# Moving the scale and offset of a norm behind the spatial mix of a gMLP layer

## The chip, the cores and the metric

The kernel runs on one core of a Trainium2 chip. The metric is the device time of one execution in microseconds (us). The engines are named as in the profile: PE multiplies matrices (TensorE), PEld loads its weights, DVE is the vector engine, ACT the scalar engine, POOL is GpSimd, and SP issues nearly all DMAs, in the order of its queue. Each engine works through its own queue in order and waits on semaphores for the others.

## The reference

The program is one inference step of a two-layer decoder, for a prompt of 512 tokens and 8 samples of 8 tokens (576 columns in all), model width 1024. Layer 0 has two attention groups, layer 1 a gMLP; each is followed by a feed-forward network with a short convolution. Only the gMLP matters here:

```
z = gelu(h @ w_in)                              # 1024 -> 4096 columns
u, v = split(z, 2, axis=-1)                     # 2048 each
v = (v - mean(v)) * rsqrt(var(v) + eps) * g + b     # g, b: one per feature (lnv_g, lnv_b)
vg = v.reshape(B, T // 128, 128, 8, 256)        # chunks of 128 positions, 8 groups of features
mixed = einsum('gts,bnsgc->bntgc', w_s * tri, vg) + b_s.T[:, :, None]
out = (u * mixed) @ w_out
```

`w_s` is a causal 128x128 matrix for each group. The normalised v (with g and b) of the 64 sample tokens is an output as well.

## The kernel before

All matrix products with weights are made of three matmuls of halves: weights and activations are split into a rounded part (`wh`, `xh`) and the rest (`wl`, `xl`). For a tile of weights, SP loads `wr` (line 250), ACT rounds it to `wh` (line 251), and DVE or POOL subtracts to get `wl` (line 254); in the gMLP layer it is always DVE. Each of the three kinds has three buffers. Columns of tokens are worked in two parts, 0 to 255 and 256 to 575.

The function `gmlp` (line 548) runs in these stages:

- The mixing weights `ws` (prompt) and `wq` (samples) are loaded and masked by POOL (line 560), the bias `bs` is loaded.
- v is projected with tokens on partitions, in eight column blocks c of 256 (lines 572 to 602). ACT writes the GELU into `z` (128 partitions, 5 blocks of tokens, 2048 features), DVE takes statistics.
- The norm of v (lines 603 to 613): `moments` (line 446) turns the statistics into mean `mv` and inverse deviation `r` by Newton steps on DVE; then, for each of four column blocks of 512 and five token blocks, DVE subtracts and scales (line 610), DVE multiplies by the gain `gb[:, 0]` (611) and POOL adds the offset `gb[:, 1]` (612). The sample rows go out as `o_cv` (613).
- `left(c)` (line 617) projects a block of 128 features of u for all tokens: 48 matmuls of line 298 into two accumulators `acc`, each read by ACT with a GELU (621). `right(c)` (line 623) mixes the same 128 features of z over positions on PE (lines 630 and 632), adds the bias on DVE (635), multiplies by u (637), and splits the product into `gch` on ACT (740) and `gcl` on DVE (741).
- `out` (line 642) multiplies four such blocks by `w_oc` and adds to the residual `x` (line 439).

Three `left`s run ahead of the first `right`. The accumulators `acc` are a ring of four banks; the two loads `gb` have two buffers. What the order on each engine is, a scheduler decides ahead of time from its own model of durations; a call of `late` pins an instruction behind the one before it on its engine. On PE it placed the first mixes into the fourth `left`.

Of the kernel before, what the change touches and what calls it, by code (L numbers as in the profile page):

```python
# [10 lines left out]
F32 = mybir.dt.float32  # L11
F32R = mybir.dt.float32r
I32 = mybir.dt.int32
AF = mybir.ActivationFunctionType
OP = mybir.AluOpType
# [3 lines left out]
P = 128  # L19
# [3 lines left out]
NS = 64  # L23
# [15 lines left out]
GB = 2  # L39
# [163 lines left out]
class Net:  # L203
# [344 lines left out]
    def gmlp(self, x, last, psum, pool, xp, *norm):  # L548

        nc, a, xs, xn = self.nc, self.a, last.xs, last.xn  # L550
        g1 = self.plus_one(1, 2, xp, "g1")

        ws = pool.tile([P, 8, P], F32, name="ws")
        wq = pool.tile([NS, 8, NS], F32, name="wq")
        for t, src, mask in ((ws, "wsT", "c_triT"), (wq, "wsS", "c_triB")):
            n = t.shape[0]
            self.late(nc.sync.dma_start(t, a[src]))
            tri = xp.tile([P, T], F32, name="tmp", bufs=3)[:n, :n]
            self.late(nc.sync.dma_start(tri, a[mask]))
            nc.gpsimd.tensor_tensor(t, t, tri[:, None, :].to_broadcast([n, 8, n]), op=OP.mult)  # L560
        bs = pool.tile([P, 8, P], F32, name="bs")
        self.late(nc.sync.dma_start(bs, self.rows(a["bs"], P).rearrange("p (g t) -> p g t", g=8)))

        z = pool.tile([P, 5, 2 * D], F32, name="z", bufs=1)
        st = pool.tile([P, 5, 8, 6], F32, name="zst")
        self.late(nc.gpsimd.memset(st[NS:, 4], 1.0))
        self.late(nc.gpsimd.memset(z[NS:, 4], 0.0))
        todo = [(c, u) for c in range(8) for u in range(2)]
        led = {}

        def lead():
            c, u = todo.pop(0)
            if u == 0:
                led[c] = [], [psum.tile([P, 2, 256], F32, name=name, bufs=b) for name, b in (("acc", 4), ("tc", 2))]
            units, accs = led[c]
            units.append(self.weights(a["w_v"][c, u], 1024))
            self.token_unit({tb: accs[tb // 4][:, tb % 2] for tb in (2, 3, 4)}, units[u], u, 256, xs, xn, True, (2, 3, 4))


        for _ in range(3):  # L580
            lead()
        for c in range(8):
            first = None
            for u in range(2):
                if c not in led or u == len(led[c][0]):
                    lead()
                units, accs = led[c]
                first = first or psum.tile([P, 2, 256], F32, name="acc", bufs=4)
                self.token_unit([first[:, 0], first[:, 1]], units[u], u, 256, xs, xn, True, (0, 1))
            accs = [first] + led.pop(c)[1]  # L590
            for i in range(3):
                n, nb = (P, 2) if i < 2 else (NS, 1)
                zz = z[:n, 2 * i:2 * i + nb, c * 256:c * 256 + 256]
                if i < 2:
                    nc.scalar.activation(zz, accs[i], AF.Gelu)
                else:
                    self.both_halves(accs[i][:, 0], zz[:, 0])
                    nc.scalar.activation(zz, zz, AF.Gelu)
                for t in range(nb):
                    nc.vector.bn_stats(st[:n, 2 * i + t, c], zz[:, t])  # L600
            if c == 0:
                last.residual()
        mv, r = self.moments(st, pool)
        for c in range(4):
            gb = pool.tile([P, 2, 512], F32, name="gb", bufs=GB)
            self.late(nc.sync.dma_start(gb[:, 0], self.rows(a["lnvg"][:, c * 512:(c + 1) * 512], P)))
            self.late(nc.sync.dma_start(gb[:, 1], self.rows(a["lnvb"][:, c * 512:(c + 1) * 512], P)))
            for tb in range(5):
                zz = z[:, tb, c * 512:(c + 1) * 512]
                nc.vector.tensor_scalar(zz, zz, mv[:, tb, 0:1], r[:, tb:tb + 1], op0=OP.subtract, op1=OP.mult)  # L610
                nc.vector.tensor_tensor(zz, zz, gb[:, 0], op=OP.mult)
                nc.gpsimd.tensor_tensor(zz, zz, gb[:, 1], op=OP.add)
        nc.sync.dma_start(a["o_cv"], z[:NS, 4])
        mm = nc.tensor.matmul
        u = {}

        def left(c):
            wh, wl, _ = self.weights(a["w_u"][c], 1024)
            u[c] = pool.tile([P, T], F32, name="u", bufs=UA + 1)
            for part, (t0, t1) in enumerate(PARTS):  # L620
                nc.scalar.activation(u[c][:, t0:t1], self.product(psum, wh, wl, 0, xs, part), AF.Gelu)

        def right(c):
            cols = slice(c * P, (c + 1) * P)
            g = c // 2
            gt = xp.tile([P, T], F32, name="tmp", bufs=3)
            for part, (t0, t1) in enumerate(PARTS):
                mix = psum.tile([P, 512], F32, name="acc", bufs=4)
                for n in range(2):
                    mm(mix[:, n * P:(n + 1) * P], z[:, 2 * part + n, cols], ws[:, g], start=True, stop=True)  # L630
                if part:
                    mm(mix[:, 256:256 + NS], z[:NS, 4, cols], wq[:, g], start=True, stop=True)
                for o, i, n, m in ((t0, 0, 2, P), (NP, 256, 8, 8))[:1 + part]:
                    wide = lambda t: t.rearrange("p (n t) -> p n t", n=n)
                    nc.vector.tensor_tensor(wide(gt[:, o:o + n * m]), wide(mix[:, i:i + n * m]),
                                            bs[:, g, None, :m].to_broadcast([P, n, m]), op=OP.add)
            nc.vector.tensor_mul(gt, gt, u.pop(c))
            pair = tuple(t[:, c % GC] for t in ring)
            self.split_to(*pair, gt)
            return self.halves(pair)  # L640

        def out(*chunks, norm=None):
            self.accumulate(x, a["w_oc"], [(c0, [gc.pop(c) for c in range(c0, c1)]) for c0, c1 in chunks],
                            g1, psum, xp, None, norm)

        ring = self.pair(pool, [P, GC, T], "gc")
        gc = {}
        for c in range(UA):
            left(c)
        for c in range(16):  # L650
            if c + UA < 16:
                left(c + UA)
            gc[c] = right(c)
            for c0, c1 in GO[0]:
                if c1 == c + 1:
                    out((c0, c1))
        norm = Norm(self, x, *norm, psum, pool, xp, "z")
        out(*GO[1], norm=norm)
        return norm
# [862 lines left out]
def _layout(inp):  # L1522
    n = lambda k: np.asarray(inp[k])
    fm = lambda w, cols: w.reshape(w.shape[0] // P, P, w.shape[1] // cols, cols)
    d = {}
    x = np.concatenate([n("x_prompt")[0], n("x_sample").reshape(NS, D)], 0)
    d["xT"] = x.T.reshape(KB, P, T).transpose(1, 0, 2)
    c = np.concatenate([n("c_prompt"), n("c_sample")], 0)
# [13 lines left out]
    o = dict(qa=0, ka=512, va=1024, qi=1536, sm=2048, qb=2120, kb=2632, vb=3144, fb=3656)  # L1542
# [21 lines left out]
    ws = n("w_spatial")[0]  # L1564
    d["wsT"] = ws.transpose(2, 0, 1)
    d["wsS"] = np.tile(ws[:, :8, :8].transpose(2, 0, 1), (8, 1, 8))
    d["bs"] = n("b_spatial").reshape(1, 1024)
    d["lnvg"], d["lnvb"] = n("lnv_g"), n("lnv_b")
    for k, v in _consts().items():
        d["c_" + k] = v  # L1570
    return {k: np.ascontiguousarray(v) for k, v in d.items()}
# [41 lines left out]
```

## Time and profile before

| | |
|---|---|
| median of 3 runs | 1954.88 us (1953.62 to 1960.26) |
| profiled execution | 1954.99 us, span 1952.9 us |
| TensorE clock granted, mean | 0.968 |
| PE busy | 1830.8 us (94% of the span) |
| DVE busy | 1185.3 us (61%) |
| ACT busy | 736.5 us (38%) |
| POOL busy | 374.0 us (19%) |
| DMA | 284.39 MB, mean 146 GB/s |

The span runs from the first to the last instruction; the execution's own time is 2.1 us longer. Shares are averages over stages with different limits. The gMLP layer lies between about 1130 and 1510 us. Of the clock, 1.00 in a row stands for 2.4 GHz and 0.50 for 1.2 GHz.

### The profile page before, as it was taken

How to read it: one execution, taken by the hardware profiler on the slowest of the kernel's cores; microseconds unless marked ns; L12 is line 12 of the kernel's file. 1: busy time of each engine (PE TensorE's matmuls, PEld its weight loads, DVE VectorE, ACT ScalarE, POOL GpSimd, SP SyncE). 2: the span in 40 equal slices, each digit the busy share in tenths (PEclk: the TensorE clock that was granted, in tenths of full speed). 3: DMA queues.
4: the chain of work that ended last, by engine and by line, in shares of the span. 5: the costliest groups of instructions: out<-in, count | busy, mean ns of one | idle time of the engine just before them, and what ended most of it. 6: DMA issues, size and time to landing. Idle time of an engine off the chain costs nothing. (4 is left out here: it accounts for less than half of the span.)

```text
span 1952.9 us, 37037 instructions
## 1 busy us (share of the span) xinstructions
PE 1830.8 (94%) x14456; PEld 1627.1 (83%) x14456; DVE 1185.3 (61%) x2437; ACT 736.5 (38%) x1372; POOL 374.0 (19%) x521
## 2 busy tenths in 40 slices
PE   6889999898889899999999999899998999999996
PEld 4646877555559899999999899799997999999995
DVE  3549963455449754545456953875468555565577
ACT  2323222255444533424344433122224535344543
POOL 2323511110025300100012330430013201010124
PEclk9989999999899999999999999899998999999998
DMA  8446587797864345353543333321222231313242
GB/s 287 128 151 219 179 263 244 238 304 240 279 232 141 118 132 181 126 181 128 193 140 109 107 101 98 94 70 59 82 97 86 71 103 62 102 50 114 87 139 92
DMA packets 140032, 284.39 MB, mean 146 GB/s; under 512 B 32338, under 2 KB 42002, under 8 KB 139794
## 3 DMA queue, kind: packets, MB, share of 16 engines
q1 hardware_dynamic: 139138, 279.67, 43.8%
q0 software_dynamic: 720, 2.36, 0.4%
q8 instruction: 114, 1.87, 0.4%
q14 instruction: 60, 0.49, 0.1%
HBM read 271.04 MB, written 10.94 MB: 144 GB/s over the span
## 5 line engine op out<-in xcount | busy, mean ns | idle before, releaser
L298 PE MATMUL acc<-xh,wh 128*128 128x256 f32 (+1 forms) x1664 | 499.9, 301 | 3.0 <-ACT xh L161 1.7
L298 PE MATMUL acc<-xl,wh 128*128 128x256 f32 (+1 forms) x1664 | 497.5, 299 | 4.8 <-DVE xl L162 4.8
L298 PE MATMUL acc<-xh,wl 128*128 128x256 f32 (+1 forms) x1664 | 496.0, 298 | 6.0 <-DVE wl L254 6.0
L251 ACT CAST wh<-wr 128x1024 fp32r<-128x1024 f32 (+2 forms) x276 | 260.7, 949 | 536.6 <-PE acc L298 371.6
L254 DVE TENSOR_TENSOR wl<-wr,wh 128x1024 fp32r<-128x1024 f32 (+2 forms) x211 | 229.4, 1090 | 240.2 <-ACT wh L251 214.4
L298 PEld LDWEIGHTS acc<-xh,wh 128*128 128x128 f32 x1664 | 319.9, 192 | 11.5 <-issue 6.2
L298 PEld LDWEIGHTS acc<-xh,wl 128*128 128x128 f32 x1664 | 319.9, 192 | 6.6 <-DVE wl L254 6.2
L298 PEld LDWEIGHTS acc<-xl,wh 128*128 128x128 f32 x1664 | 319.9, 192 | 6.2 <-DVE xl L162 6.0
L254 POOL TENSOR_TENSOR wl<-wr,wh 128x1024 fp32r<-128x1024 f32 x65 | 160.5, 2469 | 531.2 <-ACT wh L251 513.4
L298 PE MATMUL acc<-gh,wl 128*128 128x256 f32 (+1 forms) x704 | 207.7, 298 | 1.6 <-DVE wl L254 1.6
L298 PE MATMUL acc<-gl,wh 128*128 128x256 f32 (+1 forms) x704 | 208.8, 298 | 0.0
L298 PE MATMUL acc<-gh,wh 128*128 128x256 f32 (+1 forms) x704 | 207.5, 300 | 0.4 <-ACT gh L740 0.4
L439 DVE SCALAR_TENSOR_TENSOR x<-acc,g,x 128x256 f32<-128x256 f32 x256 | 119.7, 476 | 118.3 <-PE acc L298 112.9
L525 DVE SCALAR_TENSOR_TENSOR y<-up,wc,y 128x592 f32<-128x592 f32 x176 | 150.6, 856 | 34.0 <-ACT y L522 29.9
L298 PEld LDWEIGHTS acc<-gh,wh 128*128 128x128 f32 x704 | 132.4, 189 | 5.5 <-issue 2.9
L298 PEld LDWEIGHTS acc<-gh,wl 128*128 128x128 f32 x704 | 132.6, 189 | 2.9 <-DVE wl L254 1.9
L298 PEld LDWEIGHTS acc<-gl,wh 128*128 128x128 f32 x704 | 133.3, 189 | 0.3 <-DVE gl L741 0.2
L518 POOL COPY tail<-up 128x2 f32<-128x2 f32 x88 | 26.1, 297 | 519.4 <-ACT up L516 519.1
L516 ACT COPY up<-acc 128x256 f32<-128x256 f32 x176 | 65.1, 371 | 130.0 <-PE acc L298 121.8
L283 PE MATMUL s<-wh,xh 128*128 128x256 f32 (+1 forms) x256 | 82.4, 330 | 3.2 <-ACT wh L251 3.2
L522 ACT ACTIVATE y<-up,wc 128x592 f32<-128x592 f32 x88 | 77.8, 884 | 9.2 <-POOL up L514 1.1
L285 PE MATMUL s<-wh,xl 128*128 128x256 f32 (+1 forms) x256 | 81.0, 317 | 0.0
(435 smaller groups left out, 3513.5 us busy)
## 6 DMA issues: line engine op xcount, KB each, us to landing
wr<-in_w_up SPq DMA_DIRECT2D x88, 512.0 KB
wr<-in_w_down SPq DMA_DIRECT2D x32, 512.0 KB
wh<-in_w_mod SPq DMA_DIRECT2D x30, 512.0 KB
wl<-in_w_mod SPq DMA_DIRECT2D x30, 512.0 KB
wr<-in_w_mod SPq DMA_DIRECT2D x28, 512.0 KB
own<-in_kT_b SPq DMA_DIRECT2D x48, 256.0 KB
own<-in_v_b SPq DMA_DIRECT2D x44, 256.0 KB
wr<-in_w_down SPq DMA_DIRECT2D x32, 320.0 KB
```

The source lines that it names most:

```text
L251: nc.scalar.copy(h, r)
L254: (nc.vector if low == "v" else nc.gpsimd).tensor_sub(l, r, h.bitcast(F32))
L283: mm(out, sh, mh, start=start, stop=False)
L285: mm(out, sl, mh, start=False, stop=stop)
L298: mm(acc, w[:, k * P:(k + 1) * P], m, start=i == 0, stop=i == n - 1)
L439: nc.vector.scalar_tensor_tensor(xp, acc[:, :256], g1[:, ob, 0:1], xp, op0=OP.mult, op1=OP.add)
L516: nc.scalar.copy(u[:, 2 + 256 * part:258 + 256 * part], accs[part][:, :256])
L518: nc.gpsimd.tensor_copy(tail[:, blk, 0:2], u[:, NP:NP + 2])
L522: nc.scalar.activation(y[:, :n], u[:, 0:n], AF.Identity, bias=wc[:, 3, blk:blk + 1], scale=wc[:, 0, blk:blk + 1])
L525: nc.vector.scalar_tensor_tensor(y[:, :n], u[:, k:k + n], wc[:, k, blk:blk + 1], y[:, :n], op0=OP.mult, op1=OP.add)
```

## The change

Since g and b belong to a feature, they can be taken out of the sum over positions: mixing `n * g + b` over s gives `g * mix(n) + b * sum_s w[t, s]`. So `z` is now only centred and scaled. The normalization is shared by DVE (token blocks 0, 2, 4) and ACT (blocks 1 and 3, with a `shift` of -mean * r). Two matmuls of a tile of ones with the masked `ws` give the sums of the mixing weights on all partitions (`wsum`, copied out by ACT). In `right`, DVE forms for each block of 128 features an offset tile `off = wsum * b + bs`, and the bias sum becomes `mix * g + off`. The gains and offsets come a second time as `lnvT`, one per partition. The output `o_cv` is made apart on POOL, in eight pieces of 256 features for the 64 sample rows, with loads of g and b broadcast to 64 partitions and a store for each piece.

```
+        lnv = pool.tile([P, 2, 16], F32, name="lnv")
+        self.late(nc.sync.dma_start(lnv, a["lnvT"]))
...
+        one = pool.tile([P, P], F32, name="one")
+        self.late(nc.gpsimd.memset(one, 1.0))
+        wsum = pool.tile([P, 8, P], F32, name="wsum")
+        for i in range(2):
+            ps = psum.tile([P, 4, P], F32, name="acc", bufs=4)
+            nc.tensor.matmul(ps, one, ws[:, 4 * i:4 * i + 4], start=True, stop=True)
+            nc.scalar.copy(wsum[:, 4 * i:4 * i + 4], ps)
+
         mv, r = self.moments(st, pool)
+        shift = pool.tile([P, 5], F32, name="zshift")
+        nc.vector.scalar_tensor_tensor(shift, mv[:, :, 0], -1.0, r, op0=OP.mult, op1=OP.mult)
         for c in range(4):
-            gb = pool.tile([P, 2, 512], F32, name="gb", bufs=GB)
-            self.late(nc.sync.dma_start(gb[:, 0], self.rows(a["lnvg"][:, c * 512:(c + 1) * 512], P)))
-            self.late(nc.sync.dma_start(gb[:, 1], self.rows(a["lnvb"][:, c * 512:(c + 1) * 512], P)))
             for tb in range(5):
                 zz = z[:, tb, c * 512:(c + 1) * 512]
-                nc.vector.tensor_scalar(zz, zz, mv[:, tb, 0:1], r[:, tb:tb + 1], op0=OP.subtract, op1=OP.mult)
-                nc.vector.tensor_tensor(zz, zz, gb[:, 0], op=OP.mult)
-                nc.gpsimd.tensor_tensor(zz, zz, gb[:, 1], op=OP.add)
-        nc.sync.dma_start(a["o_cv"], z[:NS, 4])
+                if tb % 2:
+                    nc.scalar.activation(zz, zz, AF.Identity, bias=shift[:, tb:tb + 1], scale=r[:, tb:tb + 1])
+                else:
+                    nc.vector.tensor_scalar(zz, zz, mv[:, tb, 0:1], r[:, tb:tb + 1], op0=OP.subtract, op1=OP.mult)
+        for c in range(8):
+            cols = slice(c * 256, c * 256 + 256)
+            gb = pool.tile([NS, 2, 256], F32, name="gb", bufs=GB)
+            for i, name in enumerate(("lnvg", "lnvb")):
+                self.late(nc.sync.dma_start(gb[:, i], self.rows(a[name][:, cols], NS)))
+            nc.gpsimd.tensor_tensor(gb[:, 0], gb[:, 0], z[:NS, 4, cols], op=OP.mult)
+            nc.gpsimd.tensor_tensor(gb[:, 0], gb[:, 0], gb[:, 1], op=OP.add)
+            nc.sync.dma_start(a["o_cv"][:, cols], gb[:, 0])
...
             gt = xp.tile([P, T], F32, name="tmp", bufs=3)
+            off = pool.tile([P, P], F32, name="goff", bufs=2)
+            nc.vector.scalar_tensor_tensor(off, wsum[:, g], lnv[:, 1, c:c + 1], bs[:, g], op0=OP.mult, op1=OP.add)
...
-                    nc.vector.tensor_tensor(wide(gt[:, o:o + n * m]), wide(mix[:, i:i + n * m]),
-                                            bs[:, g, None, :m].to_broadcast([P, n, m]), op=OP.add)
+                    nc.vector.scalar_tensor_tensor(wide(gt[:, o:o + n * m]), wide(mix[:, i:i + n * m]), lnv[:, 0, c:c + 1],
+                                                   off[:, None, :m].to_broadcast([P, n, m]), op0=OP.mult, op1=OP.add)
```

The scheduler now sets another order in this stage; outside of the gMLP layer no engine's order changes. On DVE, behind the Newton steps, the order before was this (`wl<-wr,wh` are the remainders of the weights, `z<-z,mv,rsy` the normalization, `tmp<-acc,bs` the bias sum):

```order
L610 TENSOR_SCALAR z<-z,mv,rsy 128x512 x9
L611 TENSOR_TENSOR z<-z,gb 128x512
L610 TENSOR_SCALAR z<-z,mv,rsy 128x512 x5
L611 TENSOR_TENSOR z<-z,gb 128x512 x8
L610 TENSOR_SCALAR z<-z,mv,rsy 128x512
L611 TENSOR_TENSOR z<-z,gb 128x512
L610 TENSOR_SCALAR z<-z,mv,rsy 128x512 x5
L254 TENSOR_TENSOR wl<-wr,wh 128x1024 x2
L635 TENSOR_TENSOR tmp<-acc,bs 128x256
L254 TENSOR_TENSOR wl<-wr,wh 128x1024
```

Now the same place on DVE reads as follows (lines of the changed kernel, where 623 is the normalization, 616 the shift, 655 the scaled sum, 646 the offset tile):

```order
L616 SCALAR_TENSOR_TENSOR zshift<-mv,rsy 128x5
L623 TENSOR_SCALAR z<-z,mv,rsy 128x512 x12
L254 TENSOR_TENSOR wl<-wr,wh 128x1024 x3
L655 SCALAR_TENSOR_TENSOR tmp<-acc,lnv,goff 128x256
L254 TENSOR_TENSOR wl<-wr,wh 128x1024
L655 SCALAR_TENSOR_TENSOR tmp<-acc,lnv,goff 128x256
L655 SCALAR_TENSOR_TENSOR tmp<-acc,lnv,goff 128x64
L657 TENSOR_TENSOR tmp<-tmp,u 128x576
L646 SCALAR_TENSOR_TENSOR goff<-wsum,lnv,bs 128x128
L761 TENSOR_TENSOR gcl<-tmp,gch 128x576
```

The first `wl` now stands behind 12 instructions on z, before behind 30. On ACT, the two copies and the eight normalizations stand between the casts of `wh` for the third and the fourth `left`:

```order
L251 CAST wh<-wr 128x1024
L612 COPY wsum<-acc 128x512 x2
L639 ACTIVATE u<-acc 128x256
L621 ACTIVATE z<-z,zshift,rsy 128x512 x8
L251 CAST wh<-wr 128x1024
L639 ACTIVATE u<-acc 128x320
```

Before, the GELU and the casts stood there alone. On PE, the two matmuls for `wsum` come just ahead of the first `left`, and the first mix now comes behind the whole fourth `left`. On SP, the pieces of the new output stand between the loads of weights:

```order
L250 DMA wr<-in_w_u 128x1024 x6
L631 DMA o_cv<-gb 64x256
L628 DMA gb<-in_lnvg 64x256
L628 DMA gb<-in_lnvb 64x256
L631 DMA o_cv<-gb 64x256
L628 DMA gb<-in_lnvg 64x256
L628 DMA gb<-in_lnvb 64x256
L250 DMA wr<-in_w_u 128x1024
L250 DMA wr<-in_w_oc 128x512
L631 DMA o_cv<-gb 64x256
```

This pattern goes on up to the eighth `o_cv`, with three more single loads of `w_oc` in it; the fifth load of `w_oc` comes behind the eighth `o_cv`. Before, the same loads had two pairs of `gb` and one `o_cv` between them.

## Rows read from the trace of the kernel before

**Rows 1.** Busy time by stretch: stretch, its length, engines (instructions), clock, DMA share, GB/s

```profile
1130.00:1230.00 100.00, 100.00 (x808) 90.76 (x807) 46.38 (x79) 33.62 (x53) 15.54 (x12) 1.00 0.32 101
...
1250.00:1260.00 10.00, 3.97 (x24) 3.21 (x22) 10.00 (x8) 1.38 (x2) 10.00 (x7) 0.79 0.17 51
1260.00:1270.00 10.00, 7.42 (x44) 7.42 (x45) 9.97 (x11) 0.38 (x1) 6.13 (x5) 0.70 0.52 156
...
1280.00:1290.00 10.00, 7.83 (x44) 7.03 (x44) 9.23 (x11) 1.52 (x4) 5.64 (x4) 0.83 0.23 72
...
1300.00:1350.00 50.00, 50.00 (x376) 49.42 (x375) 26.56 (x59) 12.83 (x21) 0.00 (x0) 1.00 0.26 81
```

**Rows 2.** PE in order of time: start, duration, engine, line, operands, idle before

```profile
1231.96 0.28 PE L298 MATMUL acc<-xh,wh 128*128 128x256 f32 x1
...
1251.17 0.28 PE L298 MATMUL acc<-xh,wh 128*128 128x256 f32 x1
...
1252.83 0.49 PE L630 MATMUL acc<-ws,z 128*128 128x128 f32 x2 [0.52 <-POOL z L612]
1254.49 0.49 PE L630 MATMUL acc<-ws,z 128*128 128x128 f32 x2 [1.18 <-POOL z L612]
1255.90 0.69 PE L632 MATMUL acc<-wq,z 64*128 64x64 f32 x2 [0.92 <-POOL z L612]
1262.58 0.58 PE L298 MATMUL acc<-xh,wl 128*128 128x256 f32 x1 [6.00 <-DVE wl L254]
...
1286.64 2.34 PE L630 MATMUL acc<-ws,z 128*128 128x128 f32 x8 [2.17 <-DVE tmp L635]
...
1297.70 1.05 PE L630 MATMUL acc<-ws,z 128*128 128x128 f32 x8
...
1299.05 0.39 PE L298 MATMUL acc<-gch,wh 128*128 128x256 f32 x1
```

**Rows 3.** DVE in order of time, from the end of the Newton steps

```profile
1237.32 4.20 DVE L610 TENSOR_SCALAR z<-z,mv,rsy 128x512 f32<-128x512 f32 x9
...
1245.30 4.89 DVE L611 TENSOR_TENSOR z<-z,gb 128x512 f32<-128x512 f32 x8
...
1253.24 7.09 DVE L610 TENSOR_SCALAR z<-z,mv,rsy 128x512 f32<-128x512 f32 x5
1260.25 4.49 DVE L254 TENSOR_TENSOR wl<-wr,wh 128x1024 fp32r<-128x1024 f32 x2
...
1274.81 7.48 DVE L611 TENSOR_TENSOR z<-z,gb 128x512 f32<-128x512 f32 x5
```

**Rows 4.** POOL in order of time, the first stretch of its sums

```profile
1246.06 17.60 POOL L612 TENSOR_TENSOR z<-z,gb 128x512 f32<-128x512 f32 x9 [2.33 <-DVE z L611]
```

**Rows 5.** PE by stretch: length, busy (instructions), clock, DMA share, GB/s

```profile
1260.00:1262.00 2.00, 0.00 (x0) 0.50 0.01 5
...
1288.00:1290.00 2.00, 2.00 (x8) 0.50 0.75 229
```

**Rows 6.** POOL's lines 612 and 560: ns min/median/max, first and last start

```profile
L612 POOL TENSOR_TENSOR z<-z,gb x20: 1380/1727/5297, 1242.3 to 1283.4; 128x512 f32<-128x512 f32 x20
...
L560 POOL TENSOR_TENSOR wq<-wq,tmp x1: 1292/1292/1292, 1144.6 to 1144.6; 64x512 f32<-64x512 f32 x1
```

**Rows 7.** ACT by shape over the span: count, busy us, mean ns, idle before

```profile
L251 ACT CAST wh<-wr 128x1024 fp32r<-128x1024 f32 x204 | 213.3, 1048 | 366.8 <-PE acc L298 212.0 <-DMA wr<-in_w_aa 34.5 <-DMA wr<-in_w_v 30.8
...
L134 ACT ACTIVATE z<-z,shift,rsy 128x512 f32<-128x512 f32 x4 | 3.0, 808 | 3.2 <-DVE shift L124 3.2
```

**Rows 8.** An f32 matmul of 512 columns, and DVE's scaled sum from PSUM

```profile
L1122 PE MATMUL o<-relu,i_c_selh x16: 592/595/1219, 105.9 to 126.3; 128*128 128x512 f32 x16
...
L439 DVE SCALAR_TENSOR_TENSOR x<-acc,g,x 128x256 f32<-128x256 f32 x256 | 119.7, 476 | 118.3 <-PE acc L298 112.9
```

**Rows 9.** SP's queue: a load of gb, and the store of o_cv

```profile
1255.87 0.33 SPq L606 DMA_DIRECT2D gb<-in_lnvg  x1
...
1287.63 0.51 SPq L613 DMA_DIRECT2D o_cv<-z  x1
```

More of the change, by code (lines that the diff above doesn't have):

```diff
@@ L1568, in _layout @@
     d["lnvg"], d["lnvb"] = n("lnv_g"), n("lnv_b")
+    d["lnvT"] = np.stack([n("lnv_g"), n("lnv_b")], 1).reshape(2, 16, P).transpose(2, 0, 1)
     for k, v in _consts().items():
```

## The prediction

> **What bounds it now.** I read a table of busy time by stretch around the gMLP layer first [rows 1]. While v is projected (1130 to 1230) PE is busy for all 100 us at full clock; from 1300 it is again. So a change counts only where PE stands still or runs slow. Between them lie two holes: 3.97 us busy of 10 from 1250, and 7.83 of 10 from 1280, with clocks of 0.79, 0.70 and 0.83. In both, DVE is busy for 9 to 10 us of 10. Then PE in order of time [rows 2]. The u projections ("lefts") run from 1231.96. After 1251 the first spatial mix waits three times for POOL's z (0.52, 1.18, 0.92). At 1256 PE begins 6.00 us of waiting for wl of line 254, a DVE instruction, and at 1286.64 it has waited 2.17 us for DVE's tmp. Idle time sums to 10.79 us. Last DVE and POOL [rows 3, 4]. DVE's queue holds 20 subtractions and scalings of z (line 610) and 20 products with gb (611), and POOL 20 sums with gb (612). The wl that PE waits for stands behind them on DVE. POOL's running sums also stretch DVE: line 610 takes 4.20/9 = 0.47 us without POOL and 7.09/5 = 1.42 beside it.
>
> The price of the two holes is the gap between what PE had to do and the time it took, up to the first matmul of the output projection (gch, 1299.05). From 1231.96 that is 67.09 us. The work in it is seven lefts and four mixes (c = 0 to 3; three lefts run ahead). Three lefts undisturbed last 1251.17 - 1231.96 = 19.21, so one is 6.40; a mix is 1299.05 - 1297.70 = 1.35 [rows 2]. 7 x 6.40 + 4 x 1.35 = 50.2. So 16.9 us are lost: 10.8 idle, the other 6.1 mostly half clock. The clock stood at 0.50 (1.2 GHz) in the idle time at 1260 to 1262, and again at 1288 to 1290 behind the second wait [rows 5]; the work done in such stretches takes twice as long.
>
> **The change part by part.** *Removed from DVE:* 20 products of 0.61 (4.89/8) to 1.50 us (7.48/5) and 8 of 20 normalizations. Kept are 12 of 0.47, or 1.42 beside POOL [rows 3]. *Removed from POOL:* 20 sums over 128x512. Added are 16 operations over 64x256. The nearest row is 64x512 at 1.29 us [rows 6], so about 0.65 each, 10 us in all, and no mix depends on them.
>
> *Moved to ACT:* 8 normalizations. The same form (line 134) takes 0.808 [rows 7], 6.5 us in all, and two copies of 128x512, priced like that row, 1.6 at most.
>
> *Added on PE:* two f32 matmuls over 512 columns, ahead of the lefts. An f32 matmul is two passes in the trace (a mix has four and stands as x8 in rows 2). A pass at the pace of a left (24 matmuls of 576 columns in all in 6.40, 0.46 ns a column) is 0.24; the isolated row of that shape says 0.595 [rows 8]. Four passes are 0.9 to 2.4. I take 0.9, since PE is streaming there. Their two accumulators come from the same four banks and push the later ones on by two. PE went through those banks without a wait up to 1251 [rows 2], so I cost this at nothing; uncovered it is one read by ACT, 0.8 by rows 7. What they multiply, the masked weights, POOL makes long before, at about 1144 (line 560 [rows 6]). One load of 16 KB goes ahead of the w_v loads: nothing, since PE is busy through that whole stretch [rows 1].
>
> *Added on DVE:* 16 offsets of 128x128, two ahead of the normalization and 14 in the loop. Nearest is the 128x256 form, 0.476 [rows 8], so 0.25 to 0.48, 4 to 8 us over the loop, where DVE is busy 26.56 of 50 [rows 1]. Each stands before gcl, at a point where DVE waits for ACT's cast anyway: nothing. The bias sum becomes a scaled sum of the same size, also covered.
>
> *What is late next.* In the new order PE meets the mixes only after four whole lefts. Its times, with 0.9 us added: left 1 at 1239.3, left 2 at 1245.7, left 3 at 1252.1, first mix at 1258.5, output projection at 1283.1. DVE's Newton steps end at 1237.3 [rows 3]; two offsets and the new shift make it 1238.0. DVE: 12 x 0.47 ends at 1243.7 (all 12 beside POOL: 1255.0). ACT: 8 x 0.808 ends at 1244.5. Behind these stands the cast wh of left 3 on ACT (1.05 [rows 7]), 1245.6, and its wl on DVE (2.25 by row 1260.25 of rows 3, the dear case), 1247.9 against a need at 1252.1. Closer is an accumulator: the second part of left 2 reuses the bank of left 0's second part, whose GELU stands behind the cast on ACT: done 1246.0, needed at 1245.7 + 6.40 x 256/576 = 1248.6. Slack 2.6 us, the smallest I find. The mix needs z at 1258.5, 14 us after ACT is done.
>
> *Sum:* 16.9 - 0.9 = 16.0 us. The profiled execution took 1954.99 (span 1952.9 and 2.1 around it), 0.1 above the median of the runs. Forecast 1939.0.
>
> **Two rules weighed.** Beside POOL a normalization takes 1.42 us against 0.47 [rows 3]. The Trainium skill (SBUF — State Buffer, Who interferes with whom) says that a DVE copy, cast or tensor_scalar in a two-port mode and a GpSimd instruction shut each other out for a whole instruction, while one with at most one SBUF input does not contend. By that, each POOL operation under way costs one of the 12 normalizations at most its own length, and the new sum from PSUM costs nothing; the trace's 0.95 us of stretch beside 1.4 us sums agrees in size. It would make rival C real only if all POOL work falls into the 6 us.
>
> The gb loads of before, two of 256 KB issued from 1255.87 on, had left the engines nearly empty by 1260 to 1262 (DMA share 0.01): 4.1 us, and I use 4.4 with something for the signal [rows 5, 9]. The Trainium skill (DMA: Bandwidth & Descriptors, Rules for kernel authors) says that under 64 KB a transfer is mostly overhead, and its section on latency puts the fixed part at about 2 us. That speaks against cutting one store and eight loads into 24 transfers of 64 KB. By it a step of the chain below would be an estimated 1.3 + 1.3 + 2.0 = 4.6 us, where a landing of a quarter of the bytes in a quarter of the time would make it 3.7.
>
> **Rivals.** *A, the SP queue holds up the weights.* The o_cv chain now is 8 steps: gb loaded, POOL twice, o_cv out; SP issues in order, a gb waits behind the o_cv before it, and the w_oc loads stand between them. A step is three issues (0.33 to 0.51 each [rows 9], 1.0 to 1.5), two POOL operations (2 x 0.65 = 1.3, at worst half of the 17.60/9 = 1.96 of rows 4 each, 2.0) and a landing of 1.1 (a quarter of the bytes in a quarter of the 4.4 us) to 4.4. That is 3.4 to 7.9; I take 4.8 (1.3, 1.3, and half of the 4.4 for one of the two loads). The first o_cv can go at 1240.7, behind DVE's third normalization and two POOL operations; the eighth goes seven steps later, and the fifth w_oc right behind it. A unit of w_oc lasts half a left, 3.2 us, so the fifth is needed at 1283.1 + 12.8 = 1295.9, less some 4.5 for load (half of 4.4), cast and wl: issue by 1291.4. It decides from (1291.4 - 1240.7)/7 = 7.2 us a step; at 7.9 PE waits 4.6 us: 1943.6. For it: 24 transfers, each pair waiting for the one before. Against: 34 us at my value, 51 available. *B, ACT is late.* If the 8 normalizations took over 1.14 us each, PE would wait for the bank; at 1.5 by 2.9 us: 1942. The rows of that form average 0.808 [rows 7]. *C, DVE is stretched.* All 12 at 1.42 put wl of left 3 at 1257.3, 5 us late, and some 2 us of half clock after it: 1946. Only POOL operations of the first steps fall into that time, a few of 0.65. *D, the time is given back:* the output projection would run into its weights. From 1300 on DMA share is 0.26 and PE never starves [rows 1], so a shift of the start shifts the end; 1950 if two thirds came back. *E, the slower side:* the same chain as in A with POOL held off by DVE as at its worst. With POOL at 2.65 us an operation (half of the longest sum, 5.30 [rows 6]) a step is 1.3 + 5.3 + 4.4 = 11.0, and PE waits 77 - 51 = 26 us for w_oc in the middle of the projection: 1965. It is slower than before from (50.7 + 16)/7 = 9.5 us a step. POOL's 5.30 was met once in 20, with DVE's queue full of two-input products that are now gone.
>
> **Chances.** Forecast 0.80 (1935.5 to 1942); A 0.07; B 0.03; C 0.04; D 0.04; E 0.02. Range 1935 to 1946: below for a loss that I may have sized too small (its half-clock part is a remainder) and the spread of runs, above to A, B and C; D and E are left out. A measurement of this kernel can tell about 0.3%, 5.9 us, from no change, so "faster" is below 1949.0: the forecast, A, B and C, 0.94. "Same" is D, 0.04, "slower" E, 0.02.
>
> **What would show it.** Right: PE busy 10 of 10 at clock 1.00 from 1232 to 1300, the first gch matmul near 1283, four f32 passes before the first left of about 0.24 us each. DVE done with z near 1244 to 1246, ACT near 1245, no wait of PE for line 254 or for z. The o_cv steps 4 to 6 us apart on SP, the last before 1291. Wrong: a wait of PE for ACT's u in left 2 (B), for wl in left 3 (C), or for wl of w_oc with SP waiting for POOL (A, E); or the gch matmul early but the end not (D).

## The result and the profile after

The changed kernel takes 1943.09 us (median of 6 runs, 1936.08 to 1947.28) against 1954.56 (6 runs, 1950.94 to 1960.26): a ratio of 0.9937, 95% interval 0.9917 to 0.9956, or 12.3 us by the ratio. Taken again beside the experiments it gave 0.9925 (0.9904 to 0.9946). The forecast was 1939.0, the range 1935 to 1946.

The profiled execution took 1944.53 us. Its span divides at two matmuls on PE: the first one behind the v projection, and the first `gch` matmul of the output projection.

| us | before | after | difference |
|---|---|---|---|
| start of the span to the end of the v projection | 1231.96 | 1234.91 | +2.95 |
| from there to the first `gch` matmul ("the gap") | 67.09 | 52.17 | -14.92 |
| from there to the end ("the tail") | 653.85 | 655.72 | +1.87 |
| span | 1952.9 | 1942.8 | -10.1 |

The first line lies ahead of nearly all that was changed. In the ten profiles of this document it is anything from 1226.5 to 1234.9 us, so it is the spread of runs. The other two sum to 13.05 us, or 0.67%, within both intervals; the second is the change, and the third is taken up again in the part on the prediction.

The busy time by stretch of the kernel after, with the columns of [rows 1]:

```profile
1130.00:1230.00 100.00, 100.00 (x809) 91.17 (x808) 44.74 (x74) 32.58 (x51) 15.68 (x13) 1.00 0.29 94
...
1250.00:1260.00 10.00, 10.00 (x78) 10.00 (x77) 2.45 (x2) 3.00 (x6) 2.52 (x5) 1.00 0.43 118
1260.00:1270.00 10.00, 10.00 (x75) 9.81 (x74) 4.54 (x7) 2.44 (x4) 3.07 (x3) 1.00 0.22 65
1280.00:1290.00 10.00, 10.00 (x76) 9.81 (x76) 6.01 (x12) 2.69 (x5) 1.61 (x2) 1.00 0.31 89
1300.00:1350.00 50.00, 50.00 (x375) 49.25 (x374) 25.32 (x53) 12.92 (x22) 0.00 (x0) 1.00 0.22 71
```

Both holes are closed. DVE, busy for 9 to 10 us of 10 before, now is for 2.45 to 6.01. PE in order of time, to be held against [rows 2]:

```profile
1234.91 1.88 PE L611 MATMUL acc<-ws,one 128*128 128x512 f32 x4
1236.22 0.68 PE L298 MATMUL acc<-xh,wh 128*128 128x256 f32 x1
1236.74 0.28 PE L298 MATMUL acc<-xl,wh 128*128 128x256 f32 x1
...
1243.01 0.28 PE L298 MATMUL acc<-xh,wh 128*128 128x256 f32 x1
...
1262.21 1.05 PE L650 MATMUL acc<-ws,z 128*128 128x128 f32 x8
...
1287.08 0.38 PE L298 MATMUL acc<-gch,wh 128*128 128x256 f32 x1
```

From the first left to the first `gch` matmul no row of PE has a wait. The four passes for `wsum` take 1.31 us to the start of the next matmul, and that one's successor comes 0.52 later where the others come 0.12 apart: the first left lasts 6.79 us, the next ones 6.40. Now DVE (to be held against [rows 3]), ACT and POOL:

```profile
1240.72 6.41 DVE L623 TENSOR_SCALAR z<-z,mv,rsy 128x512 f32<-128x512 f32 x12
1247.58 1.22 DVE L254 TENSOR_TENSOR wl<-wr,wh 128x1024 fp32r<-128x1024 f32 x1 [0.45 <-ACT wh L251]
...
1265.86 0.82 DVE L646 SCALAR_TENSOR_TENSOR goff<-wsum,lnv,bs 128x128 f32<-128x128 f32 x1
```

```profile
1240.84 5.76 ACT L621 ACTIVATE z<-z,zshift,rsy 128x512 f32<-128x512 f32 x8 [0.77 <-DVE zshift L616]
1246.51 1.04 ACT L251 CAST wh<-wr 128x1024 fp32r<-128x1024 f32 x1
1247.45 0.69 ACT L639 ACTIVATE u<-acc 128x320 f32<-128x320 f32 x2
...
```

```profile
1242.31 0.91 POOL L629 TENSOR_TENSOR gb<-gb,z 64x256 f32<-64x256 f32 x1 [91.48 <-DVE z L623]
1243.30 0.80 POOL L630 TENSOR_TENSOR gb<-gb 64x256 f32<-64x256 f32 x1
1247.86 1.54 POOL L629 TENSOR_TENSOR gb<-gb,z 64x256 f32<-64x256 f32 x1 [3.75 <-DMA gb<-in_lnvg]
...
1253.60 0.73 POOL L629 TENSOR_TENSOR gb<-gb,z 64x256 f32<-64x256 f32 x1 [3.39 <-DMA gb<-in_lnvg]
```

DVE's next `wl` waits for ACT's cast, no longer for DVE's own queue. And SP, the stores of `o_cv` and the loads of `w_oc`, the first two and the last:

```profile
1244.13 0.51 SPq L631 DMA_DIRECT2D o_cv<-gb  x1
1250.23 0.49 SPq L631 DMA_DIRECT2D o_cv<-gb  x1
...
1282.06 0.49 SPq L631 DMA_DIRECT2D o_cv<-gb  x1
1282.67 13.85 SPq L250 DMA_DIRECT2D wr<-in_w_oc  x4
```

A step of that chain is (1282.06 - 1244.13) / 7 = 5.42 us.

### The profile page after: what moved, and what is told of

It reads as the page before. It is cut to its first block, busy times and chain, and to the rows that moved or that the text cites. A ratio compares the mean times of both kernels' runs of the same rounds, so it can differ in the third digit from the quotient of the medians.

```text
span 1942.8 us, 37068 instructions
## 1 busy us (share of the span) xinstructions
PE 1826.5 (94%) x14460; PEld 1622.8 (84%) x14460; DVE 1157.8 (60%) x2426; ACT 743.7 (38%) x1382; POOL 351.3 (18%) x518
## 3 DMA queue, kind: packets, MB, share of 16 engines
q8 instruction: 114, 1.87, 0.4%
## 5 line engine op out<-in xcount | busy, mean ns | idle before, releaser
L298 PEld LDWEIGHTS acc<-xh,wh 128*128 128x128 f32 x1664 | 318.2, 191 | 11.7 <-issue 6.4
```

The source lines that it names most:

```text
L298: mm(acc, w[:, k * P:(k + 1) * P], m, start=i == 0, stop=i == n - 1)
```

## The experiments

Gap and tail below are those of the table, each from the one profile of the run.

**The changed kernel again, and the normalization left on DVE.** In the second, `if tb % 2:` became `if tb > 4:`, so ACT takes none of the blocks and DVE all 20.

> The changed kernel as it is. S is the time on PE from the end of the v projection to the first matmul of the output projection (gch); it was 67.1 us before and 52.2 in the changed kernel's first profile. Theory (the holes on PE are closed, and that is all): S 52 to 52.5 again, and a full time 13 to 16 us under the kernel before, the spread of single runs coming from the part ahead of the gMLP layer, which is the same code. Rival (part of the gain is given back behind the stage): S 52, but the full time only 8 to 11 us under before, with a longer stretch from the first gch to the end, by 3 us or more.

> The changed kernel with all 20 normalizations on DVE and none on ACT. Theory (what counted was that the products and sums with gain and offset left the tokens): DVE ends z 4 us later than with ACT's help, at 10 to 11 us after the shift, still ahead of the need for wl of the fourth left; S 52 to 53, full time as the changed kernel within 1 us. Rival (ACT's share was the gain): PE waits for wl of line 254 in the fourth left by 3 us or more, S 56 to 60, full time 4 to 8 us over the changed kernel.

The repetition gave 1940.38 us, 0.9925 (0.9904 to 0.9946), a gap of 52.17 and a tail of 655.9. That is 14.7 us under before by the ratio, as the theory had it; the tail is 2 us longer than before, short of the rival's 3. With all 20 on DVE it was 1942.16, 0.9927 (0.9909 to 0.9945), a gap of 52.17 and a tail of 655.64: to the hundredth the gap of the changed kernel. (The time is 1.8 us over the repetition, where 1 was expected; the intervals overlap almost wholly.) DVE's rows there:

```profile
1232.31 10.06 DVE L623 TENSOR_SCALAR z<-z,mv,rsy 128x512 f32<-128x512 f32 x20
1242.30 2.35 DVE L254 TENSOR_TENSOR wl<-wr,wh 128x1024 fp32r<-128x1024 f32 x2
```

20 of them end 10 us behind the Newton steps and `wl` follows in time. ACT's share is worth nothing in the gap, since DVE had room for it once the rest was gone.

**ACT's share alone.** The kernel before, with blocks 1 and 3 normalized on ACT as in the change, gain and offset still on all tokens:

```
...
-                nc.vector.tensor_scalar(zz, zz, mv[:, tb, 0:1], r[:, tb:tb + 1], op0=OP.subtract, op1=OP.mult)
+                if tb % 2:
+                    nc.scalar.activation(zz, zz, AF.Identity, bias=shift[:, tb:tb + 1], scale=r[:, tb:tb + 1])
+                else:
+                    nc.vector.tensor_scalar(zz, zz, mv[:, tb, 0:1], r[:, tb:tb + 1], op0=OP.subtract, op1=OP.mult)
                 nc.vector.tensor_tensor(zz, zz, gb[:, 0], op=OP.mult)
                 nc.gpsimd.tensor_tensor(zz, zz, gb[:, 1], op=OP.add)
```

> The kernel before with only the token blocks 1 and 3 normalized on ACT; gain and offset stay on all tokens (20 products on DVE, 20 sums on POOL, no sums of weights on PE). Theory (products and sums were the cost): PE still waits for POOL's z in the first mixes and for wl behind DVE's products; S 58 to 65, full time 2 to 8 us under before. Rival (ACT's share was the gain): S 51 to 53, full time 14 to 16 us under before.

1949.34 us, 0.9958 (0.994 to 0.9976), a gap of 63.33: 3.76 us less than before. By the ratio the time is 8.2 us less (4.7 to 11.7), a little over the 2 to 8 of the theory; gap and tail of the one profile together are 4.7 less, and no profile shows where more would lie. DVE in order of time, and what PE waited for between 1226 and 1300 (cause, sum in us, times, longest):

```profile
1246.61 13.11 DVE L616 TENSOR_TENSOR z<-z,gb 128x512 f32<-128x512 f32 x9
1259.64 4.50 DVE L254 TENSOR_TENSOR wl<-wr,wh 128x1024 fp32r<-128x1024 f32 x2
```

```profile
PE acc L298 <- DVE wl L254: 7.5, 1, 7.5
PE acc L635 <- DVE tmp L640: 1.2, 1, 1.2
PE acc L298 <- ACT u L626: 0.6, 1, 0.6
```

The eight are off DVE's queue, but the products, now at 1.46 us each beside POOL, fill it up again to 1259.64. That is 25.5 us behind the end of the v projection (1234.10 in this profile), where `wl` came 28.3 us behind it before (1260.25 [rows 3] and 1231.96).

**The order alone.** The kernel before with all its work, but with the last three of the four blocks of the norm written behind mixes 0, 4 and 8:

```
-        for c in range(4):
+        def normed(c):
...
+        normed(0)
...
+            if c in (0, 4, 8):
+                normed(c // 4 + 1)
```

> The kernel before with all its work, but the column blocks 1 to 3 of the norm of v written behind the mixes 0, 4 and 8 instead of ahead of the lefts, which moves many products behind the first wl on DVE; nothing else changes. Rival O (it was the order, not the amount of work: wl and the first sums stood behind work that is not needed before 1300): S 51 to 56, full time 10 to 16 us under before. Theory W (the work itself had to go): DVE and POOL still cannot deliver wl and z in time, S 62 to 67, full time within 5 us of before.

1944.23 us, 0.9942 (0.9923 to 0.996). So rival O came out and theory W did not: with all the work still done, the gap is 52.65, nearly as with the change. But the tail is 660.19. The busy time by stretch shows where it comes back:

```profile
1300.00:1350.00 50.00, 47.19 (x351) 46.26 (x351) 28.67 (x49) 12.31 (x21) 8.20 (x5) 1.00 0.20 65
1350.00:1400.00 50.00, 47.67 (x346) 46.92 (x346) 32.50 (x63) 12.44 (x20) 8.08 (x5) 0.97 0.34 101
```

What PE waited for between 1300 and 1400 (cause, sum in us, times, longest), where the kernel before has no such wait:

```profile
PE acc L298 <- DVE gst L442: 5.1, 2, 2.8
```

The first of the two:

```profile
1307.42 0.38 PE L298 MATMUL acc<-gch,wh 128*128 128x320 f32 x1 [2.81 <-DVE gst L442]
```

PE stands still where the later blocks of the norm run on DVE: the read that frees the accumulator (line 442) stands behind five products in DVE's queue, which the first time take 6.38 us from 1300.37 on. Of the 14.4 us that the gap lost, 6.3 came back. This is the outcome of my rival D, time given back in the tail, but not its mechanism, since no wait is for weights. By the times of the runs alone this kernel and the changed one are not told apart: the intervals around 0.9942 and 0.9925 overlap.

**Which of the two, sums or products?** The kernel before twice more: without POOL's 20 sums, and without DVE's 20 products.

```
-                nc.gpsimd.tensor_tensor(zz, zz, gb[:, 1], op=OP.add)
```

> The kernel before without POOL's 20 sums of the offset (line 612): z lacks the offset, all else stays, DVE's 20 normalizations and 20 products among it. Theory 1 (the hole is POOL's doing: its running sums stretch DVE's instructions and PE waits for its z): 20 normalizations of 0.47 and the 10 products that stand ahead of the first wl at 0.61 end at 15.5 us behind the Newton steps, wl comes about 2 us late at most, no instruction of DVE on z is over 0.7 us, and the gap (67.09 before, 50.2 without any loss) is 51 to 54. Theory 2 (it is the amount of work on DVE, with POOL only a part): the gap stays at 58 or above.

```
-                nc.vector.tensor_tensor(zz, zz, gb[:, 0], op=OP.mult)
```

> The kernel before without DVE's 20 products of the gain (line 611): z lacks the gain, POOL's 20 sums over 128x512 stay and follow each normalization directly. By theory 1 of the run without the sums (POOL's running sums stretch DVE) the 20 normalizations stand at up to 1.42 us each beside POOL, 28 us where all of them do, wl comes up to 14 us late and the gap is 58 to 65. By the amount of DVE's work alone: 20 x 0.47 = 9.4 us, wl is early, and only the mixes wait for POOL's z: a gap of 51 to 54. The changed kernel has neither sums nor products on the tokens, and the gap there is 52.17, of which 1.7 is the new matmuls.

Without the sums: a gap of 51.17 (span 1934.9, 1936.84 us in one run), although DVE still does 20 normalizations and 20 products. Without the products: a gap of 62.84 (span 1949.3, 1951.32 us in one run). The rows of z by shape (count, busy us, mean ns), DVE's two without the sums:

```profile
L611 DVE TENSOR_TENSOR z<-z,gb 128x512 f32<-128x512 f32 x20 | 12.4, 683 | 0.0
L610 DVE TENSOR_SCALAR z<-z,mv,rsy 128x512 f32<-128x512 f32 x20 | 9.5, 542 | 0.0
```

and the same two in the kernel before, between 1230 and 1300:

```profile
L611 DVE TENSOR_TENSOR z<-z,gb 128x512 f32<-128x512 f32 x20 | 21.2, 1118 | 0.0
L610 DVE TENSOR_SCALAR z<-z,mv,rsy 128x512 f32<-128x512 f32 x20 | 16.2, 872 | 0.0
```

The same 40 instructions are 37.4 us long beside POOL's sums and 21.9 without. DVE's order up to the first `wl` is the same as before, 20 normalizations and 10 products ahead of it; without the sums it comes 15.2 us behind the Newton steps (their end is the start of the first row), before it was 22.9 [rows 3]:

```profile
1234.91 4.20 DVE L610 TENSOR_SCALAR z<-z,mv,rsy 128x512 f32<-128x512 f32 x9
...
1250.07 2.35 DVE L254 TENSOR_TENSOR wl<-wr,wh 128x1024 fp32r<-128x1024 f32 x2
```

And without the products, the normalization alone on DVE, with POOL's sums behind it, still is late:

```profile
1238.09 23.75 DVE L610 TENSOR_SCALAR z<-z,mv,rsy 128x512 f32<-128x512 f32 x20
1261.76 3.48 DVE L254 TENSOR_TENSOR wl<-wr,wh 128x1024 fp32r<-128x1024 f32 x3
```

```profile
1263.03 0.58 PE L298 MATMUL acc<-xh,wl 128*128 128x256 f32 x1 [10.17 <-DVE wl L254]
```

1.19 us each, for 0.47 undisturbed. So POOL's sums made the holes, for the most part by lengthening DVE's queue; 2.6 us of PE's waits before were for POOL's `z` itself [rows 2]. The Trainium skill (SBUF — State Buffer, Who interferes with whom) says that a DVE instruction with two SBUF inputs contends with a GpSimd instruction that reads SBUF, and that one in a two-port mode contends too. By that rule the products must get longer beside POOL, and the normalizations if they run in such a mode, which no row names; the trace shows both longer, 1118 ns against 683 for the products and 872 against 542 for the normalizations.

**The two f32 matmuls.** The changed kernel, with `wsum` copied from the masked weights in place of the matmuls:

```
-        one = pool.tile([P, P], F32, name="one")
-        self.late(nc.gpsimd.memset(one, 1.0))
...
-            ps = psum.tile([P, 4, P], F32, name="acc", bufs=4)
-            nc.tensor.matmul(ps, one, ws[:, 4 * i:4 * i + 4], start=True, stop=True)
-            nc.scalar.copy(wsum[:, 4 * i:4 * i + 4], ps)
+            nc.scalar.copy(wsum[:, 4 * i:4 * i + 4], ws[:, 4 * i:4 * i + 4])
```

> The changed kernel with the two f32 matmuls and their accumulators left out: wsum is copied by ACT from the masked mixing weights themselves, so the offsets are not the reference's. All else as in the changed kernel. In the profile of the changed kernel the four passes last 1.88 us by the row (1.31 us from the first pass to the first matmul of left 1), and the first left takes 6.79 us where the next three take 6.40. Theory (the term of my sum was sized too small: 1.7 us, not 0.9): the gap from the end of the v projection to the first gch matmul falls from 52.17 to 50.4 to 50.5 us, seven lefts of 6.40 and four mixes of 1.35 and nothing else. Rival (the 0.39 us of the first left is something else at the start of that stage, as the switch of weights): the gap falls only to 50.9.

The gap fell to 50.47: they cost 1.70 us, the 0.39 of the first left included (span 1935.5, tail 654.0, 1937.34 us in one run). Seven lefts of 6.40 and four mixes of 1.35 are 50.2, so no more than 0.3 us is left to gain there.

**A longer chain on SP.** The changed kernel with `o_cv` in 16 pieces:

```
-        for c in range(8):
-            cols = slice(c * 256, c * 256 + 256)
-            gb = pool.tile([NS, 2, 256], F32, name="gb", bufs=GB)
+        for c in range(16):
+            cols = slice(c * 128, c * 128 + 128)
+            gb = pool.tile([NS, 2, 128], F32, name="gb", bufs=GB)
```

> The changed kernel with the samples' v written out in 16 pieces of 128 features in place of 8 of 256; all the same output. The chain on SP (gains and offsets loaded, POOL twice, store) has 16 steps; the eighth w_oc load stands behind the 15th store and the next w_u behind the 16th. With 8 pieces a step took 5.4 us. Theory A (a step is mostly fixed: issue, transfer and signal; half the bytes make it 4.8 to 5.2 us): the 16th store goes 15 steps behind the first at about 1244, at 1316 to 1322, the next w_u had to be issued by about 1307, PE waits for weights in the output projection for 9 to 15 us and some half clock after it: 1953 to 1961 us, ratio 0.999 to 1.003 to the kernel before: the whole gain is gone. Theory B (a step goes with the bytes: 2.7 to 3.4 us): the 16th store goes by 1295, no wait of PE, 1941 to 1944 us as the changed kernel.

1951.79 us (10 runs), 0.9994 (0.998 to 1.0008): the whole gain is gone, as by theory A. The time is a little below the 1953 to 1961 given there: the 16th store went out at 1308.54 instead of 1316 to 1322. The gap is 52.17, the tail 665.61, 9.9 more than with eight pieces. SP, then ACT, DVE and PE around the second of two holes:

```profile
1297.30 0.53 SPq L250 DMA_DIRECT2D wr<-in_w_oc  x1
...
1304.13 0.49 SPq L631 DMA_DIRECT2D o_cv<-gb  x1
...
1305.94 1.06 SPq L250 DMA_DIRECT2D wr<-in_w_oc  x2
```

```profile
1309.52 1.30 ACT L251 CAST wh<-wr 128x512 fp32r<-128x512 f32 x2 [8.29 <-DMA wr<-in_w_oc]
```

```profile
1310.17 0.69 DVE L254 TENSOR_TENSOR wl<-wr,wh 128x512 fp32r<-128x512 f32 x1 [7.17 <-ACT wh L251]
1310.78 0.22 DVE L444 TENSOR_TENSOR x<-x,gst 128x64 f32<-128x64 f32 x1
1310.92 0.87 DVE L439 SCALAR_TENSOR_TENSOR x<-acc,g,x 128x256 f32<-128x256 f32 x2
```

```profile
1302.63 0.35 PE L298 MATMUL acc<-gch,wh 128*128 128x256 f32 x1 [2.76 <-DVE x L439]
...
1311.54 0.55 PE L298 MATMUL acc<-gch,wh 128*128 128x256 f32 x1 [3.96 <-DVE x L439]
```

PE's row names DVE's `x` of line 439, the last that it waited for, which frees the accumulator. But that instruction stood behind `wl` in DVE's queue, `wl` waited for ACT's cast, the cast for `w_oc`, and `w_oc` for the 15th piece's turn on SP. A wait has to be followed past the name in its row. Halving the bytes brought a step from 5.42 to (1308.54 - 1240.19) / 15 = 4.56 us, less than theory A's 4.8 to 5.2 and far from theory B's 2.7 to 3.4. From the start of a load of `lnvg` on SP's queue to POOL's instruction that reads it there are 2.88 us with 64 KB and 2.63 with 32 KB (medians of 7 and 15 loads). The Trainium skill (DMA: Bandwidth & Descriptors, Rules for kernel authors) says that under 64 KB one pays mostly overhead; the trace agrees: with half the bytes 91% of that time is left.

## Why the prediction was right, and where it was off

The mechanism is the one forecast: PE's holes closed because `wl` no longer stands behind work stretched by POOL. The time lies in the range, 4.1 us above the forecast. It is 1.1 us above the band that the forecast itself was given, 1935.5 to 1942, in the part of the range that was kept for A to C, and PE had none of their waits; the repetition, 1940.38, lies in the band. So that the first measurement fell into the range is owed in part to its width. By the steps:

- *The price of the holes, 16.9 us.* Right: without the f32 matmuls the gap is 50.47 against the 50.2 worked out from lefts and mixes, 16.6 less than before. Of the 16.0 us forecast the gap gave 14.92: 0.8 went to the f32 matmuls of the next point, and 0.3 is what the 50.2 left out.
- *The two f32 matmuls, 0.9 us.* Mis-sized: 1.70. I took a pass at the pace of the lefts, 0.46 ns a column. The mixes, f32 themselves and in [rows 2], have 8 x 128 columns in 1.05 us, 1.03 ns a column or 2.1 us for four passes of 512. Measured were 0.64 ns a column and 0.39 us on the next left, between the two. The upper bound of 2.4 was kept for the range, but the value came from the wrong kind of row.
- *A shift of the start shifts the end.* Off by 1.87 us: rival D's outcome on a small scale, not its mechanism, as PE waits for no weights in the output projection. Counted from the first `gch` matmul, PE in the kernel after is up to 0.5 us ahead through the first 150 us. It falls behind between 150 and 225 us, around the end of the gMLP layer, and is 0.8 to 0.9 behind from there on. At its last wait for `wl`, which is the same 1.6 us in both (1931.84 and 1920.71), it is 0.84 behind, and 1.18 at its last transposes (1938.55 and 1927.76). Between those two points the clock stays at half for longer in this pair of profiles. The last 20 us in which PE works, before and after, each 621.8 to 641.8 us behind the first `gch` matmul:

```profile
1920.87:1940.87 20.00, 12.67 (x84) 11.46 (x82) 15.48 (x23) 5.62 (x9) 11.42 (x7) 0.83 0.20 66
```

```profile
1908.90:1928.90 20.00, 14.58 (x91) 13.27 (x90) 15.15 (x21) 5.46 (x9) 12.26 (x7) 0.74 0.20 66
```

  The clock of these 20 us does not sort the kernels, though: it is 0.83 in the repetition and with all 20 on DVE, which have the long tail too. The last 0.6 us lies behind DVE's last instruction: from its end to the end of the span it is 4.13 to 4.16 us in the four kernels with `o_cv` in eight pieces, and 3.52 to 3.53 in the six others. The tail is 655.6 to 655.9 in the three profiles with the f32 matmuls and eight pieces, and 652.9 to 654.2 in the kernel before and four others without holes of their own in the tail. Why is not settled; no run was made for it.
- *Work taken off DVE and POOL.* The total was right, but I put DVE's 20 products first and POOL's stretch second, and gave ACT's share as a part of the gain. One at a time, against the gap before, the sums are worth 15.9 us, the products 4.3 and ACT's share 3.8, and beside the others ACT's share is worth 0.00. The three do not add up, since each shortens the same queue. Nor did the work have to go for the gap to close: written later, it left a gap of 52.65, and the change has 52.17, of which 1.70 are its f32 matmuls.
- *DVE and ACT have time.* Right: DVE's 12 took 6.41 us (5.7 forecast), ACT's eight 5.76 (6.5). The smallest slack, the accumulator of left 2, came out at 4.4 us instead of 2.6: the GELU of left 0's second part ends at 1247.87, and the second part of left 2 starts at 1252.29, 2.88 us behind the first.
- *Offsets hidden.* Right, though one of them takes up to 0.82 us, not 0.48 at most: DVE has the time, and PE does not wait for it.
- *Rival A and E, the chain on SP.* A step is 5.42 us instead of 4.8, mainly as POOL's two operations take 0.91 and 0.83 on average in place of 0.65. The fifth `w_oc` went out at 1282.67; the limit, moved to the measured first `gch` matmul, is 1287.08 + 8.3 = 1295.4. So 12.7 us were to spare. The mechanism is real: 16 steps of 4.56 run past it and cost all of the gain.
- *Rivals B and C.* PE waited neither for `u` nor for `wl`. What C describes was there in small: two of the 12 normalizations took 0.97 and 0.96 us instead of 0.54 beside POOL's first two operations, 0.8 us in all.

## What to carry to other kernels

Before pricing work that two engines do on the same data, ask how long the same instruction takes when the other engine is still: here the cheap-looking part, sums on an engine that is busy for 19% of the span, lengthened its neighbour's queue by 15.5 us, and leaving out the sums alone was worth 15.9 us in the gap, where the whole change gave 14.9. Then ask whether the work has to go or only to stand behind what others wait for: moved later, in the one placement that was run, it closed the holes too but opened two smaller ones. And a row for a new operation should be of its own data type: f32 matmuls beside it told more than the fast ones that it streams with.

## What was not expected of the hardware

Two f32 matmuls of 512 columns among the others cost more than their own 1.31 us: the left behind them took 6.79 us instead of 6.40. A load-compute-store step of 64 KB pieces took 5.42 us, and one of 32 KB pieces 4.56.
